# A hybrid decoder layer on one core: modulation loads issued by GpSimd's queue, later table clearing on VectorE

## The chip, the cores and the metric

The kernel runs on one core of a Trainium2 chip. The metric is device time in microseconds, the median of several runs; lower is better. The engines of the core are TensorE (PE in the profile, its weight loads PEld), VectorE (DVE), ScalarE (ACT), GpSimd (POOL) and SyncE (SP), whose instructions here are only the issues of transfers. Each engine works through its own instructions in order and waits at one until what it needs is there.

## What is computed

One layer of a decoder trunk in float32 for 256 tokens of width 2048. A conditioning vector `c` gives six modulation vectors, three for each of the two sub-layers; everything else depends on them sooner or later.

```
mod = silu(c) @ w_ada + b_ada                  # 2048 x 12288 weights, 100 MB
sh1, sc1, g1, sh2, sc2, g2 = split(mod, 6)
h = rms_norm(x, norm1_g) * (1 + sc1) + sh1
q, k, v, u = split(h @ w_in)                   # attention heads and state-space channels
attn = dilated_attention(rms_norm(q), rms_norm(k), v)
y = gelu(s5_mixer(u, ...)); ssm = y * sigmoid(y @ w_glu + b_glu)
x = x + g1 * (concat(rms_norm(attn), rms_norm(ssm)) @ w_out)
h2 = rms_norm(x, norm2_g) * (1 + sc2) + sh2
x = x + g2 * (square(relu(h2 @ w_ff1)) @ w_ff2)
```

## The kernel before, in words

**Weights.** A weight tile of 128 x 2 x 512 float32 (0.5 MB) is loaded into a slot of the tag `raw`, of which there are five (`RAW`, `raw` at L176 to L179). `load_w` and, from `w_out` on, `load_p` split it into a rounded high part `wh` on ScalarE (L161) and the remainder `wl` on VectorE (L136), each with three buffers; the matmuls (L193 to L195, L860 to L872) use both. A `raw` slot is free again when VectorE has written `wl`.

**Modulation.** The 12288 columns of `w_ada` are 24 blocks of 512, each of four pieces of 1 MB (`ada_pieces`, L246). For eight of the blocks (`PE_BLOCKS`) TensorE multiplies the pieces by the padded vector `cpad` (L254). For the others VectorE multiplies a piece by the broadcast vector `cbc` in place and sums it up (L158). `ada_raw` (L232) fetches a piece. The first eight pieces go into eight halves and wholes of tiles that are not in use yet (`first`: Q, K, U, V, TO, CA; L236). Later pieces go into the tag whose turn it is in `ring["tags"]`, a list that changes from stage to stage (`RINGS`): either a large tile that is free in that stage, as one load of 1 MB (L242), or `T0` or `raw`, as two loads of half a piece each (L244 and L178). In the second case modulation and weights share the five `raw` slots.

**The order.** `pump` (L285) advances the modulation by pieces, and `pump_at(i)` calls it between pieces of the main work at a rate from the list `PUMPS`; where a value of `mod` is needed, `pump(99, until=...)` brings it up to there. The main work is, in order: the norm of x, `make_h` and the input projection in parts (`w_in_block`, `w_in_pair`), the tables of the state space between them (`b_step`, `ca_step`, `wb_block`, `toep_half`), the scan (`state_in`, `scan`), attention and `w_glu`, `w_out`, and from about 525 us the feed-forward part (`ff1_half`, `ff1`, `ff2`). The program is written in this order; a planner then lays out each engine's own sequence from it, with its own idea of how long everything takes and of when a buffer is free, and adds the waits. All transfers are issued by the sync queue.

**Clearing.** Some tables hold zeros between written parts. GpSimd clears PD, WB0 and WB1 at the very start (L481), three parts of `toep` in the tile TO once the modulation pieces in it are used (L601), `wpad` in PD later (L492) and one column of the scan's state H in XT (L544). ScalarE then copies parts into them (`pad_write`, `toep_half`). Beyond these and four constants GpSimd has no instructions.

The functions that the change touches, with the line numbers of the profile:

Of the kernel before, what the change touches and what calls it, by code (L numbers as in the profile page):

```python
# [25 lines left out]
NB = 512  # L26
# [14 lines left out]
SUB = [0, 2, 1, 3]  # L41
# [75 lines left out]
class _K:  # L117
# [5 lines left out]
    def t(self, tag, shape, dt=F32, bufs=1):  # L123
        self.n += 1
        return self.sb.tile(list(shape), dt, name=f"{tag}_{self.n}", tag=tag, bufs=bufs)
# [5 lines left out]
    def tr(self):  # L131
        self.n += 1
        return self.ps.tile([P, NB], F32, name=f"tr_{self.n}", tag="tr", bufs=4)
# [26 lines left out]
    def copy(self, out, a, scale=1.0):  # L160
        self.last_act = self.nc.scalar.activation(out, a, AF.Copy, scale=scale).ins  # L161
# [11 lines left out]
        self.copy(hi, v)  # L173
        return self.sub(lo, v, hi.bitcast(F32))

    def raw(self, src, tag="raw"):  # L176
        raw = self.t(tag, [P, 2, NB], bufs=RAW if tag == "raw" else 1)
        self.nc.sync.dma_start(raw, src)  # L178
        return raw  # L179

    def load_w(self, src):
        parts = []
        for j in range(2):
            raw = self.raw(src[:, 2 * j : 2 * j + 2])
            hi = self.t("wh", [P, 2, NB], F32R, bufs=3)
            lo = self.t("wl", [P, 2, NB], F32R, bufs=3)
            self.split(hi, lo, raw)
            parts.append((hi, lo))
        return lambda kk: (parts[kk // 2][0][:, kk % 2, :], parts[kk // 2][1][:, kk % 2, :])
# [8 lines left out]
def _body(nc, tc, I, out, sb, ps):  # L198
    k = _K(nc, tc, I, out, (sb, ps))
# [32 lines left out]
    def ada_raw(src):  # L232
        if ring["first"] < 8:
            raw = first[ring["first"]]
            ring["first"] += 1
            nc.sync.dma_start(raw, src.rearrange("p (a n) -> p a n", a=4))  # L236
            return [raw]
        ring["i"] += 1
        tag = ring["tags"][ring["i"] % len(ring["tags"])]
        if tag not in ("raw", "T0"):  # L240
            raw = t(tag, [P, 4, NB])
            nc.sync.dma_start(raw, src.rearrange("p (a n) -> p a n", a=4))  # L242
            return [raw]
        return [k.raw(src[:, 2 * NB * i : 2 * NB * i + 2 * NB].rearrange("p (a n) -> p a n", a=2), tag) for i in range(2)]  # L244

    def ada_pieces(b):  # L246
        c4 = slice(4 * b, 4 * b + 4)
        if b in PE_BLOCKS:
            acc = tr()
            for g in range(4):  # L250
                q = 0
                for raw in ada_raw(I["w_ada"][b, g]):
                    for i in range(raw.shape[1]):
                        k.last_ada = mm(  # L254
                            acc[32 * q : 32 * q + 32, :], cpad[:, 4 * g + q, :], raw[:, i, :],
                            start=g == 0, stop=g == 3,
                        ).ins
                        q += 1
                if g < 3:
                    yield  # L260
# [6 lines left out]
        else:  # L267
            part = t("adap", [P, 2, 4], bufs=2)
            for j in range(4):
                o = 0  # L270
                for i, raw in enumerate(ada_raw(I["w_ada"][b, j])):
                    n = raw.shape[1] * NB
                    rf = raw.rearrange("p a n -> p (a n)")
                    stt(rf, rf, 1.0, cbc[:, o : o + n], ALU.mult, ALU.mult, accum=part[:, i, j : j + 1])
                    o += n
                if i:
                    add(part[:, 0, j : j + 1], part[:, 0, j : j + 1], part[:, 1, j : j + 1])
                if j < 3:
                    yield
# [94 lines left out]
    s5 = {}  # L374
# [97 lines left out]
    def pad_write(dst, src):  # L472
        for gp in range(2):
            pr = slice(64 * gp, 64 * gp + 64)
            copy(dst(gp)[pr], src[pr])
# [13 lines left out]
    def wb_block(i):  # L489
        if i == 0:  # L490
            s5["wpad"] = t("PD", [P, 8, 2, 4, 2, 16])
            nc.gpsimd.memset(s5["wpad"], 0.0)  # L492
        wpad, w, rr = s5["wpad"], i // 2, slice(8 * (i % 2), 8 * (i % 2) + 8)
        for b in range(4):
            pad_write(lambda gp: wpad[:, :, :, b, gp, :], by_r(bpow[w][:, 3 - SUB[b], :, rr]))
        wb.append(t(f"WB{i}", [P, 8, 2, P]))
        for r in range(0, 8, 2):
            pt = tr()
            for e in range(4):
                src = wpad[:, r + e // 2, e % 2].rearrange("p s g j -> p (s g j)")  # L500
                nc.tensor.transpose(pt[:, P * e : P * e + P], src, ident)
            copy(wb[i][:, r : r + 2].rearrange("p r i n -> p (r i n)"), pt)
# [38 lines left out]

    def state_in():
        H = t("XT", [P, 2, 32, 64])
        nc.gpsimd.memset(H[:, :, :, 0:1].rearrange("p i r c -> p i (r c)"), 0.0)  # L544
        for r2 in range(0, 32, 4):
            pt = tr()
            pv = pt.rearrange("p (r i c) -> p r i c", r=4, i=2)
            for r in range(r2, r2 + 4):
                for ri in range(2):
                    mm(pv[:, r - r2, ri], wb[r // 8][:, r % 8, ri], u2[:, :, r, :], start=True, stop=True)  # L550
            copy(H[:, :, r2 : r2 + 4, 1:64].rearrange("p i r c -> p r i c"), pv[:, :, :, 0:63])
        return H
# [45 lines left out]
    toep = t("TO", [P, 32, 2, 4, 16])  # L598
    for b in range(1, 4):
        tz = toep[32 * b : 32 * b + 32].rearrange("p r g s j -> p (r g) (s j)")  # L600
        nc.gpsimd.memset(tz[:, :, 0 : 16 * SUB[b]], 0.0)  # L601
    ca = t("CA", [P, 32, 2, 4, 16])
    with tc.issue_after(h_end):
        for w in range(2):
# [27 lines left out]
    for w in range(2):  # L632
        run(w_in_block(2 + w, [0, 1]), 2)
        with tc.issue_after(h_end):
            for d in range(1, 4):
                b_step(d, w, cw[:, 0], cw[:, 1])
        wb_block(2 * w)
        wb_block(2 * w + 1)
# [15 lines left out]
    for ch in range(2):  # L654
        nc.vector.transpose(u2[:, ch].rearrange("p r c -> p (r c)"), accs["u"][:, ch])
    H = state_in()
    scan()
    for n in (4, 5, 2, 3):
# [140 lines left out]
    for n in range(2):  # L799
        pz = [p[:, 0:SEQ] for p in (k.acc(), k.acc(), k.acc(), k.acc())]  # L800
        for kg in range(2):
            w = k.load_w(I["w_glu"][kg, n])
            pump_at(10)
            for kk in range(4):
                c = 4 * kg + kk
# [208 lines left out]
def _build(arrays):  # L1014
    nc = bacc.Bacc("TRN2", target_bir_lowering=False, num_devices=1)
    I = {
        n: nc.dram_tensor(n, a.shape, mybir.dt.from_np(a.dtype), kind="ExternalInput").ap() for n, a in arrays.items()
    }
    out = nc.dram_tensor("out_0_dram", (16, P, SEQ), F32, kind="ExternalOutput").ap()
    with tile.TileContext(nc, schedule_with_timeline_sim=True) as tc:  # L1020
        with tc.tile_pool(name="sb", bufs=1) as sb, tc.tile_pool(name="ps", bufs=1, space=PSUM) as ps:
            _body(nc, tc, I, out, sb, ps)
    return nc
# [9 lines left out]
```

## Time and profile before

| | |
|---|---|
| median of 3 runs | 1296.64 us (1294.19 to 1296.89) |
| the profiled execution | 1291.11 us, span 1289.3 us |
| TensorE busy | 1193.7 us, 93% |
| VectorE busy | 910.5 us, 71% |
| ScalarE busy | 579.0 us, 45% |
| GpSimd busy | 13.0 us, 1%, 12 instructions |
| bytes moved | 299.64 MB, mean 232 GB/s |
| mean granted clock of TensorE | 0.948 |

The rows come from one profiled execution, all times in microseconds from its start. A group of instructions is named by line, engine, operation and by `out<-in`, the tiles that it writes and reads. "idle before" is the time that the engine stood still in front of an instruction, with the one that ended it. In the chain of waits each step is followed back from the last instruction to what released it; "issue" there is time for which the profile shows no wait. A share of the chain tells where the end of the program was decided, a share of busy time only how much an engine did. Issues of transfers are short; the time to landing, from issue to the last byte, is given beside them.

### The profile page before, as it was taken

To read this page: it belongs to the slowest core of one execution; us is meant where nothing else is said; L and a number is where in the kernel's file an instruction comes from. 1 tells how busy PE (TensorE), PEld (TensorE's weight loads), DVE (VectorE), ACT (ScalarE), POOL (GpSimd) and SP (SyncE) were. 2 spreads that over 40 slices of the span, in tenths; PEclk is the share of its full clock that TensorE was granted. 3 is DMA by queue.
4 is the path that set the end of the run, shared out by engine and by line. 5 is a ranking of instruction groups with operands and counts; after the bars stand their busy time and mean duration, and the time that the engine had idled before them with its cause. 6 is when DMAs were issued, how large, how long until landed. Compare 5 with 4: busy or idle time off the path is not lost.

```text
span 1289.3 us, 18892 instructions
## 1 busy us (share of the span) xinstructions
PE 1193.7 (93%) x7330; PEld 1012.5 (79%) x7330; DVE 910.5 (71%) x1499; ACT 579.0 (45%) x792; POOL 13.0 (1%) x12
## 2 busy tenths in 40 slices
PE   4688899998998799789989999999999999999998
PEld 1456677863777699789978888888888888888887
DVE  5977697899534985668799655975576666667564
ACT  3588644332145544334354444453344443344432
POOL 1100000000000000000000000000000000000000
PEclk9798999997679899989999999999999999999999
DMA  9785898779155665658997666766677666767663
GB/s 371 286 317 186 280 333 287 274 267 385 36 179 180 239 193 175 210 182 297 327 326 252 203 191 216 262 212 182 195 236 240 225 187 190 219 222 227 202 212 95
DMA packets 77705, 299.64 MB, mean 232 GB/s; under 512 B 8624, under 2 KB 10928, under 8 KB 71856
## 3 DMA queue, kind: packets, MB, share of 16 engines
q1 hardware_dynamic: 77616, 298.45, 69.1%
q8 instruction: 57, 0.93, 0.3%
q14 instruction: 32, 0.26, 0.0%
HBM read 296.31 MB, written 2.10 MB: 231 GB/s over the span
## 4 chain that ended last, share of the span: by engine, by line
PE 60%; DMA 15%; DVE 15%; ACT 5%; issue 4%; SPq 0%; ACTq 0%; DVEq 0%
PE acc L860 31%; PE acc L862 15%; DMA raw<-w_ada 10%; DVE wl L136 4%; DVE raw L158 3%; DVE T L136 2%; PE acc L872 2%; PE acc L870 2%; PE acc L869 2%; PE acc L701 1%; DMA raw<-w_ff 1%; ACT wh L161 1%; PE acc L697 1%; DVE XT L136 1%; ACT TO L161 1%
## 5 line engine op out<-in xcount | busy, mean ns | idle before, releaser
L161 ACT ACTIVATE wh<-raw 128x1024 fp32r<-128x1024 f32 x360 | 381.3, 1060 | 502.1 <-PE acc L860 290.8
L136 DVE TENSOR_TENSOR wl<-raw,wh 128x1024 fp32r<-128x1024 f32 x360 | 439.7, 1223 | 219.0 <-ACT wh L161 217.2
L158 DVE SCALAR_TENSOR_TENSOR raw<-raw,cbc 128x1024 f32<-128x1024 f32 x98 | 119.6, 1225 | 49.3 <-DMA raw<-w_ada 49.0
L860 PE MATMUL acc<-CA,wh 128*128 128x512 f32 x512 | 139.7, 398 | 6.4 <-DVE rows L136 3.4
L860 PEld LDWEIGHTS acc<-CA,wh 128*128 128x128 f32 x512 | 88.4, 190 | 19.2 <-ACT wh L161 4.5
L862 PEld LDWEIGHTS acc<-CA,wl 128*128 128x128 f32 x512 | 76.7, 189 | 10.7
L862 PE MATMUL acc<-CA,wl 128*128 128x256 f32 x512 | 78.2, 278 | 0.0
L860 PE MATMUL acc<-WB,wh 128*128 128x512 f32 x256 | 70.2, 396 | 0.0
L860 PE MATMUL acc<-TO,wh 128*128 128x512 f32 x256 | 70.0, 394 | 0.0
L193 PE MATMUL acc<-wh,HA 128*128 128x512 f32 x128 | 49.8, 417 | 13.2 <-ACT HA L161 9.2
L194 PE MATMUL acc<-wl,HB 128*128 128x512 f32 x128 | 52.6, 411 | 7.1 <-DVE wl L136 7.0
L194 PE MATMUL acc<-wl,HA 128*128 128x512 f32 x128 | 53.2, 416 | 0.9 <-DVE wl L136 0.9
L195 PE MATMUL acc<-wh,HB 128*128 128x512 f32 x128 | 50.6, 400 | 0.0
L195 PE MATMUL acc<-wh,HA 128*128 128x512 f32 x128 | 50.5, 406 | 0.0
L193 PE MATMUL acc<-wh,HB 128*128 128x512 f32 x128 | 47.5, 403 | 1.7 <-ACT wh L161 1.7
L860 PEld LDWEIGHTS acc<-WB,wh 128*128 128x128 f32 x256 | 43.5, 188 | 5.6
L860 PEld LDWEIGHTS acc<-TO,wh 128*128 128x128 f32 x256 | 43.4, 188 | 5.5
L862 PEld LDWEIGHTS acc<-WB,wl 128*128 128x128 f32 x256 | 39.1, 188 | 5.9
L862 PEld LDWEIGHTS acc<-TO,wl 128*128 128x128 f32 x256 | 38.9, 188 | 5.8
L193 PEld LDWEIGHTS acc<-wh,HA 128*128 128x128 f32 x128 | 25.1, 198 | 22.4 <-ACT HA L161 9.3
L862 PE MATMUL acc<-WB,wl 128*128 128x256 f32 x256 | 40.8, 281 | 0.0
L862 PE MATMUL acc<-TO,wl 128*128 128x256 f32 x256 | 39.8, 277 | 0.0
(322 smaller groups left out, 2352.0 us busy)
## 6 DMA issues: line engine op xcount, KB each, us to landing
raw<-w_ff SPq DMA_DIRECT2D x256, 512.0 KB, 4.3
raw<-w_ada SPq DMA_DIRECT2D x98, 512.0 KB, 5.2
raw<-w_in SPq DMA_DIRECT2D x64, 512.0 KB, 6.0
raw<-w_out SPq DMA_DIRECT2D x32, 512.0 KB, 3.8
HA<-w_ada SPq DMA_DIRECT2D x11, 1024.0 KB, 7.3
PD<-w_ada SPq DMA_DIRECT2D x9, 1024.0 KB, 4.9
Q<-w_ada SPq DMA_DIRECT2D x5, 1024.0 KB, 10.3
K<-w_ada SPq DMA_DIRECT2D x5, 1024.0 KB, 8.7
```

Source lines behind the costliest of these rows:

```text
L136: return (eng or self.nc.vector).tensor_tensor(out, a, b, op=op)
L158: self.nc.vector.scalar_tensor_tensor(out, a, s, b, op0=op0, op1=op1, accum_out=accum)
L161: self.last_act = self.nc.scalar.activation(out, a, AF.Copy, scale=scale).ins
L193: mm(ps, xh, wh, start=start, stop=False)
L194: mm(ps, xh, wl, start=False, stop=False)
L195: mm(ps, xl, wh, start=False, stop=stop)
L697: mm(pv[:, r - r8], toep[:, r].rearrange("p g s j -> p (g s j)"), u2[:, :, r, :], start=True, stop=False)
L860: mm(pp[e], hi[:, e, kk], xs[kk].rearrange("p s n -> p (s n)"), start=first and kk == 0, stop=False)
L862: mm(pp[e][:, 0:SEQ], lo[:, e, kk], xs[kk][:, 0], start=False, stop=last and kk == 3)
L869: mm(o, hi[:, e, kk], xs[kk][:, 0], start=first and e + kk == 0, stop=False)
L870: mm(o, hi[:, e, kk], xs[kk][:, 1], start=False, stop=False)
L872: mm(o, lo[:, e, kk], xs[kk][:, 0], start=False, stop=last and e + kk == 4)
```

## The change

Three places in `ada_raw` and its helper `raw` issue the loads of `w_ada` on GpSimd's queue in place of the sync queue. All other transfers (x, the weights, constants, the result) stay on the sync queue. Three clearings, of `wpad`, of the column of H and of the parts of `toep`, go from GpSimd to VectorE; the clearing of PD, WB0 and WB1 at the start stays on GpSimd. Sizes, buffers, rings and rates stay as they were.

```diff
--- before.py
+++ after.py
@@ -173,9 +173,9 @@
         self.copy(hi, v)
         return self.sub(lo, v, hi.bitcast(F32))
 
-    def raw(self, src, tag="raw"):
+    def raw(self, src, tag="raw", eng=None):
         raw = self.t(tag, [P, 2, NB], bufs=RAW if tag == "raw" else 1)
-        self.nc.sync.dma_start(raw, src)
+        (eng or self.nc.sync).dma_start(raw, src)
         return raw
 
     def load_w(self, src):
@@ -233,15 +233,15 @@
         if ring["first"] < 8:
             raw = first[ring["first"]]
             ring["first"] += 1
-            nc.sync.dma_start(raw, src.rearrange("p (a n) -> p a n", a=4))
+            nc.gpsimd.dma_start(raw, src.rearrange("p (a n) -> p a n", a=4))
             return [raw]
         ring["i"] += 1
         tag = ring["tags"][ring["i"] % len(ring["tags"])]
         if tag not in ("raw", "T0"):
             raw = t(tag, [P, 4, NB])
-            nc.sync.dma_start(raw, src.rearrange("p (a n) -> p a n", a=4))
+            nc.gpsimd.dma_start(raw, src.rearrange("p (a n) -> p a n", a=4))
             return [raw]
-        return [k.raw(src[:, 2 * NB * i : 2 * NB * i + 2 * NB].rearrange("p (a n) -> p a n", a=2), tag) for i in range(2)]
+        return [k.raw(src[:, 2 * NB * i : 2 * NB * i + 2 * NB].rearrange("p (a n) -> p a n", a=2), tag, nc.gpsimd) for i in range(2)]
 
     def ada_pieces(b):
         c4 = slice(4 * b, 4 * b + 4)
@@ -489,7 +489,7 @@
     def wb_block(i):
         if i == 0:
             s5["wpad"] = t("PD", [P, 8, 2, 4, 2, 16])
-            nc.gpsimd.memset(s5["wpad"], 0.0)
+            nc.vector.memset(s5["wpad"], 0.0)
         wpad, w, rr = s5["wpad"], i // 2, slice(8 * (i % 2), 8 * (i % 2) + 8)
         for b in range(4):
             pad_write(lambda gp: wpad[:, :, :, b, gp, :], by_r(bpow[w][:, 3 - SUB[b], :, rr]))
@@ -541,7 +541,7 @@
 
     def state_in():
         H = t("XT", [P, 2, 32, 64])
-        nc.gpsimd.memset(H[:, :, :, 0:1].rearrange("p i r c -> p i (r c)"), 0.0)
+        nc.vector.memset(H[:, :, :, 0:1].rearrange("p i r c -> p i (r c)"), 0.0)
         for r2 in range(0, 32, 4):
             pt = tr()
             pv = pt.rearrange("p (r i c) -> p r i c", r=4, i=2)
@@ -598,7 +598,7 @@
     toep = t("TO", [P, 32, 2, 4, 16])
     for b in range(1, 4):
         tz = toep[32 * b : 32 * b + 32].rearrange("p r g s j -> p (r g) (s j)")
-        nc.gpsimd.memset(tz[:, :, 0 : 16 * SUB[b]], 0.0)
+        nc.vector.memset(tz[:, :, 0 : 16 * SUB[b]], 0.0)
     ca = t("CA", [P, 32, 2, 4, 16])
     with tc.issue_after(h_end):
         for w in range(2):
```

## Rows read from the trace of the kernel before

**Rows 1.** The page's first line

```profile
span 1289.3 us, 18892 instructions
```

**Rows 2.** Chain of waits over the whole span, shares by line

```profile
by line: PE acc L860 30.5%; PE acc L862 15.0%; DMA raw<-w_ada 9.6%; issue 4.4%; DVE wl L136 4.1%; DVE raw L158 2.7%; DVE T L136 2.1%; PE acc L872 1.8%; PE acc L870 1.8%; PE acc L869 1.8%; PE acc L701 1.4%; DMA raw<-w_ff 1.4%; ACT wh L161 1.
```

**Rows 3.** Stages: us; busy of PE, PEld, DVE, ACT, POOL; PEclk; DMA share; GB/s

```profile
0.00:50.00 50.00, 23.38 (x123) 9.30 (x124) 33.63 (x151) 17.48 (x36) 10.95 (x10) 0.89 0.96 381
125.00:300.00 175.00, 165.30 (x777) 129.54 (x776) 149.01 (x213) 82.08 (x115) 0.22 (x1) 0.98 0.82 288
525.00:700.00 175.00, 152.65 (x1124) 144.37 (x1124) 140.43 (x241) 73.32 (x92) 0.00 (x0) 0.94 0.80 272
700.00:1289.00 589.00, 584.37 (x3357) 509.57 (x3356) 387.22 (x521) 250.33 (x282) 0.00 (x0) 1.00 0.66 207
```

**Rows 4.** Chain of waits by line, in 125 to 300 and 525 to 700 us

```profile
by line: DMA raw<-w_ada 32.9%; issue 14.3%; DVE wl L136 12.6%; DVE raw L158 8.7%; DVE T L136 6.7%; DMA raw<-w_in 6.7%; DMA raw<-w_glu 5.7%; DVE XT L136 2.6%; DVE PD L158 2.2%; DVE WB L158 1.3%; ACT wh L161 1.2%; DVE T L158 1.2%; DVE PD L655
...
by line: DMA raw<-w_ada 32.8%; PE acc L860 11.7%; DMA raw<-w_ff 10.4%; DVE raw L158 10.2%; DVE wl L136 9.0%; issue 7.0%; PE acc L862 4.8%; ACT wh L161 3.1%; PE tr L869 2.2%; PE tr L870 2.0%; DVE rows L156 1.5%; PE tr L872 0.8%; DVE XT L156 
```

**Rows 5.** Chain of waits, 584 to 591 us: start, length, what

```profile
584.34 1.24 DVE raw L158 x2
...
585.60 5.39 DMA raw<-w_ada
```

**Rows 6.** Timeline of the sync queue: start, us, issue

```profile
584.45 1.48 SPq L178 DMA_DIRECT2D raw<-w_ada  x2
586.73 1.53 SPq L178 DMA_DIRECT2D raw<-w_ff  x2
```

**Rows 7.** The sync queue's waits, 565 to 655 us: total, times, longest

```profile
SPq L178 <- DVE wl L136: 24.4, 20, 2.3
SPq L178 <- DVE raw L158: 21.3, 21, 2.3
```

**Rows 8.** DMA issues of the page (median to landing), and issues of L178

```profile
raw<-w_ada SPq DMA_DIRECT2D x98, 512.0 KB, 5.2
...
L178 SPq DMA_DIRECT2D raw<-w_ada x98: 327/328/507, 62.7 to 1159.4; - x98
```

**Rows 9.** Timeline, clearing on POOL and DVE: start, us, idle before it

```profile
33.81 5.53 POOL L601 MEMSET TO<- 32x2048 f32 x3 [27.79 <-PE tr L254]
88.96 1.81 POOL L492 MEMSET PD<- 128x2048 f32 x1 [49.62 <-PE tr L526]
...
0.94 0.48 DVE L221 MEMSET cpad<- 128x512 f32 x1
```

**Rows 10.** Timeline of the sync queue near 410 us

```profile
410.42 0.33 SPq L178 DMA_DIRECT2D raw<-w_out  x1
410.84 11.71 SPq L242 DMA_DIRECT2D PD<-w_ada  x2
```

**Rows 11.** Timeline of VectorE and ScalarE, 68 to 78 us

```profile
68.68 1.29 DVE L136 TENSOR_TENSOR CA<-V 128x512 f32<-128x512 f32 x2
...
77.27 0.69 DVE L136 TENSOR_TENSOR cbc<-cbc,rows 128x512 f32<-128x512 f32 x1 [5.62 <-ACT rows L615]
...
70.30 3.39 ACT L161 ACTIVATE WB<-CA 64x768 f32<-64x768 f32 x4
```

**Rows 12.** Timeline of POOL and DVE, first 37 us

```profile
2.47 3.55 POOL L481 MEMSET WB<- 128x2048 f32 x2
...
3.02 3.03 DVE L152 TENSOR_SCALAR HA<-small 128x32 f32<-128x32 f32 x1 [1.42 <-DMA small<-small]
...
9.70 0.18 DVE L150 TENSOR_SCALAR HA<-HA 128x32 f32<-128x32 f32 x1
...
36.14 1.22 DVE L136 TENSOR_TENSOR wl<-raw,wh 128x1024 fp32r<-128x1024 f32 x1
```

**Rows 13.** Who waited for whom, 565 to 655 us: total, times, longest

```profile
ACT wh L161 <- DMA raw<-w_ff: 29.1, 15, 5.1
DVE raw L158 <- DMA raw<-w_ada: 11.7, 11, 3.0
```

## The prediction

> **What bounds the kernel now.** I read the page first, then the same execution by stages, then the chain of waits inside the two stages that looked loose, then the sync queue's own timeline there. The span is 1289.3 us [rows 1]. Along the chain that ended last, matmuls hold most of it, but one kind of transfer stands out: `raw<-w_ada`, the modulation loads into the five-slot ring, at 9.6% [rows 2]. The stage table says where [rows 3]. After 700 us TensorE is busy 584.37 of 589 us at a granted clock of 1.00, the 2.4 GHz level; no queue can gain there. In 125 to 300 and 525 to 700 it is busy 165.30 and 152.65 of 175 us, while the DMA engines are at 0.82 and 0.80: neither is full. In both stages a third of the chain is the same load, 32.9% and 32.8% [rows 4]. Those are the stages that this change can move, and the first 125 us, where tables are cleared.
>
> What the loose stages wait for is a ring. Modulation pieces and weights share the five `raw` slots. At 584.34 VectorE multiplies a landed piece, which frees its slot; the next load starts at 585.60 and takes 5.39 us; then again [rows 5]. The sync queue issues two modulation halves, then two weights, and the two issues of a pair, 1.48 us for both, start 1.15 us apart, which is the length of a VectorE instruction of the ring [rows 6]. The table of its waits over 565 to 655 says the same: 24.4 us for VectorE to finish a weight's low half, 21.3 us for it to finish a modulation piece [rows 7]. So the queue waits for slots to come free, in the order in which VectorE frees them. It is seldom one kind of load that holds up the other.
>
> **The change part by part, against the profiled execution.** It took 1291.11 us for a span of 1289.3; the median of the three runs is 1296.64, 5.5 us above it, and I add the sum to the median.
>
> *Modulation loads go through GpSimd.* All loads of `w_ada` move, 98 of them half pieces into the ring, with a median of 5.2 us from issue to landing; on the sync queue one issue takes 0.328 us [rows 8]. Removed from the sync queue is that issue time; it is off the chain, since the queue is waiting when it isn't issuing. Added is GpSimd's own issue, which no row shows. On the chain 9.6% of 1289.3 us is 124 us, by 5.2 us some 24 loads in a row whose length counts. Lower bound of the extra latency per load: minus 0.33 us, if GpSimd's issue were free, or minus 8 us in all. Upper bound: 1.81 us, the longest full-width GpSimd instruction [rows 9], or plus 43 us. I take 0.7 us, twice the sync queue's issue: addresses of 128 rows are far fewer words than the 2048 per partition which that clearing writes, so the price is nearer the small end. That is 17 us. Half of it I count as lost, because a load that starts later also finds less traffic in front of it (DMA share 0.8, not 1): **plus 8 us**.
>
> The Trainium skill, "DMA: Bandwidth & Descriptors", section Specifications, gives about 1 us to the first byte for a load issued by GpSimd and 0.6 us for one by the sync queue; no run here shows it yet. As an estimate from that page 24 loads would cost 10 us, and the half of them 5 us instead of my 8.
>
> *Weights alone on the sync queue.* A weight no longer stands behind a modulation load that waits, nor the other way round. In the ring this gives nothing, as read above. Among the large tiles it gives a little: at 410.42 a weight was issued that had waited, and a modulation load behind it went only 0.42 us later [rows 10]. I take minus 1 us for such places; bounds 0 and the 30 us that the second rival prices.
>
> *The start.* The DMA engines are at 0.96 and 381 GB/s in the first 50 us [rows 3]. Now modulation stands ahead of the weights in one queue; afterwards they share the engines. Five ring slots of 0.52 MB fetched meanwhile are 2.6 MB, 7 us at that rate, as the worst delay of the first eight modulation loads; against it, these no longer stand behind the 2.1 MB of `XT` (5.5 us). I take 0, with minus 5 and plus 7 as ends.
>
> *Clearing on VectorE.* Three instructions of L601 clear 64 x (16 + 32 + 48) = 6144 elements per partition; GpSimd took 5.53 us, and 1.81 us for the 2048 of L492. VectorE cleared 512 in 0.48 us [rows 9], so by that rate 5.8 and 1.9 us, and next to nothing for the 64 elements of L544. They come off GpSimd, where nothing waited for them, and join an engine which is in use. L601 needs `TO` free, which was at 33.8 us; behind it on VectorE stand the recurrence tables, the last of which (`CA`) started at 68.68 and took 1.29, and ScalarE's 3.39 us of padding read it from 70.30 on [rows 11]. So most of 5.8 us shows in ScalarE's long row of copies that follows. If they are put later, VectorE's pause of 5.62 us before 77.27 [rows 11] covers them. I take plus 4 us, bounds 0 and 7.7. L492 falls into that row of copies, which is ScalarE's, so I cost it at nothing; if VectorE is late there, its 1.9 us counts.
>
> Also, this kernel's order on every engine is laid out by a planner, which lays it out anew. I cannot see that, and put it into the width: a few us either way.
>
> Sum: 8 - 1 + 0 + 4 = plus 11 us; span about 1300, and 1296.64 + 11 = **1307.6 us**.
>
> **Rivals.** *GpSimd is locked out by VectorE.* In the first microseconds two clearings on GpSimd, 3.55 us together, ran beside a VectorE scalar operation of 128x32, which took 3.03 us where its kind takes 0.18; while L601 was cleared, a two-input subtraction took its ordinary 1.22 us [rows 12]. So the two engines do block one another, by kind of operation. If GpSimd's issues in turn waited for the VectorE instruction in progress, 24 loads would each lose up to another 1.22 us, 29 us: 1296.64 + 11 + 29 = 1337; half of it gives 1322. Against it, the ring's VectorE work is of the two-input kind that went undisturbed. Chance 0.12. The Trainium skill, "SBUF — State Buffer", section SBUF: two separate sides, states this as a rule against loads from GpSimd: while VectorE runs in a two-port mode, GpSimd can't write its descriptors and the transfer waits. The trace agrees that the port is shared (3.03 against 0.18 us), and shows it in the other direction only.
>
> *Weights run ahead: faster.* ScalarE waits 29.1 us for `raw<-w_ff` in 565 to 655 against VectorE's 11.7 us for modulation [rows 13], and of the chain in the two stages weight loads hold 6.7% and 10.4% of 175 us, 30 us [rows 4]. Had these waits come from the queue's order, separate queues would give a part back; a third is 10 us: 1296.64 - 10 = 1286.6. It decides from the point at which a weight's slot is free before the modulation loads ahead of it have been issued. Against it stand the spacing of the issues and what the queue waits for [rows 6, 7]. For it, a new order may also bring pieces forward. Chance 0.28.
>
> *Nothing shows.* The longer latency disappears in the ring's slack and the clearing in VectorE's pause: 1296.6. Against it, the loop has no slack to see [rows 5]. Chance 0.12.
>
> That the loads don't move can be left out: all three issuing lines for `w_ada` are changed, and GpSimd holds too few other instructions to be short of time.
>
> **How the numbers follow.** A measurement of this kernel can tell about 0.2%, 2.6 us, from no change. My forecast has 0.48 (its own range 1300 to 1318), the lock-out 0.12, both slower: 0.60. Nothing shows: 0.12. Weights ahead: 0.28. The range goes from 1284, which takes in most of the faster case, to 1328, where the issue price nears 1.8 us; a tenth is left out at each end.
>
> **What would show it.** Right: `raw<-w_ada` issued by GpSimd with a median to landing nearer 6 than 5.2 us; the sync queue's waits in 565 to 655 still for VectorE; TensorE busy less than 165 and 153 us per 175; three clearings of about 5.8 us on VectorE before 70 us and ScalarE's padding of `CA` later than 70.30. The last 589 us unchanged. Wrong: landings as short as before, or weights that land before ScalarE asks for them in these stages; or, for the lock-out, GpSimd's issues that end only when a VectorE instruction does.

## The result and the profile after

The changed kernel takes **1328.15 us** (median of four runs, 1323.48 to 1332.84) against 1295.41 for the kernel before (1293.43 to 1296.89, four runs): ratio 1.0254, 95% interval 1.0207 to 1.0301. It is slower by 33 us; forecast were 11, to 1307.6, and the range ended at 1328, a little below the result. The profiled execution of after took 1332.84 us, among the longer of its runs, and that of before 1291.11, so the two traces differ by 41.8 us of span; some 9 us of that are this pair's own.

The runs of the kernel before fall into two groups, 16 of 84 at 1278.6 to 1285.4 us with a mean granted clock of 0.961 to 0.968 and the others at 1289.8 to 1301.4 us with 0.943 to 0.956, so a difference of 10 us can be this and not an edit, and edits are read here by stretches of the traces, with medians as the total.

The page and the stages, of the kernel after; columns as in [rows 1, 3, 8]:

```profile
span 1331.1 us, 19023 instructions
...
raw<-w_ada POOLq DMA_DIRECT2D x98, 512.0 KB, 5.3
```

```profile
0.00:50.00 50.00, 17.10 (x66) 3.90 (x66) 23.41 (x119) 12.51 (x25) 10.79 (x17) 0.90 0.96 382
125.00:300.00 175.00, 161.67 (x765) 131.78 (x765) 140.84 (x207) 87.12 (x130) 19.02 (x36) 0.96 0.77 264
525.00:700.00 175.00, 147.46 (x1174) 143.23 (x1173) 116.40 (x190) 68.67 (x87) 19.00 (x36) 0.92 0.72 237
700.00:1331.00 631.00, 622.92 (x3563) 542.14 (x3562) 425.51 (x589) 266.69 (x300) 14.79 (x28) 1.00 0.68 211
```

```profile
L178 POOL DMA_DIRECT2D raw<-w_ada x98: 527/527/537, 84.0 to 1201.6; - x98
```

Three readings. A modulation load into the ring now costs GpSimd 0.527 us to issue, never more than 0.537, where the sync queue took 0.328 [rows 8]; from the start of the issue to landing it takes 5.3 us, before 5.2. The last stage is TensorE's as before. And the first 50 us, for which I had entered 0, hold 17.10 us of matmul where there were 23.38 [rows 3], at the same DMA share and rate.

There the trace shows what stands in the way. ScalarE, the kernel after (start, us, instruction, idle time before it and what ended that):

```profile
22.95 1.06 ACT L161 ACTIVATE wh<-raw 128x1024 fp32r<-128x1024 f32 x1 [15.44 <-DMA raw<-w_in]
26.74 1.06 ACT L161 ACTIVATE wh<-raw 128x1024 fp32r<-128x1024 f32 x1 [2.73 <-DMA raw<-w_in]
27.70 0.71 ACT L302 ACTIVATE rows<-XT 128x256 f32<-128x256 f32 x2
...
40.62 1.06 ACT L161 ACTIVATE wh<-raw 128x1024 fp32r<-128x1024 f32 x1 [9.08 <-DMA raw<-w_in]
41.58 0.71 ACT L302 ACTIVATE rows<-XT 128x256 f32<-128x256 f32 x2
...
49.30 0.42 ACT L165 ACTIVATE HB<-HB 128x256 f32<-128x256 f32 x1
```

The splits of the first weights (L161) stand among the squares of the norm (L302) and wait for their loads. The norm's square root (L165) comes at 49.30. In the kernel before it came at 31.59, behind squares that ran in one row from 21.18, and the first split followed it:

```profile
21.18 0.72 ACT L302 ACTIVATE rows<-XT 128x256 f32<-128x256 f32 x2 [15.01 <-PE tr L305]
...
31.59 0.42 ACT L165 ACTIVATE HB<-HB 128x256 f32<-128x256 f32 x1
32.09 1.06 ACT L161 ACTIVATE wh<-raw 128x1024 fp32r<-128x1024 f32 x1
```

VectorE, the kernel after, and ScalarE's wait behind it:

```profile
53.25 5.45 DVE L136 TENSOR_TENSOR XT<-XT,rbc 128x256 f32<-128x256 f32 x16
58.62 0.15 DVE L136 TENSOR_TENSOR mod<-tr,small 128x4 f32<-128x4 f32 x1
59.25 1.76 DVE L601 MEMSET TO<- 32x2048 f32 x1 [0.48 <-PE tr L254]
61.27 0.91 DVE L601 MEMSET TO<- 32x1024 f32 x1 [0.25 <-issue]
62.86 2.62 DVE L601 MEMSET TO<- 32x3072 f32 x1 [0.68 <-issue]
65.51 0.16 DVE L156 SCALAR_TENSOR_TENSOR g1c<-mod,small 128x4 f32<-128x4 f32 x1
65.59 0.15 DVE L136 TENSOR_TENSOR mod<-tr,small 128x4 f32<-128x4 f32 x1
```

```profile
65.77 2.07 ACT L324 ACTIVATE XT<-XT,mod,g1c 128x256 f32<-128x256 f32 x4 [10.03 <-DVE mod L136]
```

The clearing, 5.29 us where 5.8 was costed from [rows 9], stands between the norm and the scale `g1c`. Behind it comes the last sum for `mod`, and ScalarE waits 10.03 us until that is done before it makes the input of the first projection. So the first matmul of that projection starts at 68.21 instead of 46.40.

The whole difference by stretches, from the starts of the same instructions in each trace (us). "Scan" runs from VectorE's transposes of `u` (L655) to the first GLU matmul (L809), less the state product inside it (L701), which has its own column; "ff" from the first matmul of the attention output (L869 on `CA`) to the first of L860 on `WB`.

```
                                first   to L655  scan   L701   GLU   ff     to the
                                matmul                                      last L860
before                          46.4    181.2    110.4  34.5   54.9  294.0  563.2
after                           68.2    178.8    120.9  36.4   57.2  301.7  563.3
first 8 back on sync            56.0    174.1    119.8  36.4   58.5  301.4  562.9
clearing back on GpSimd         63.8    175.2    118.1  36.4   58.3  300.4  563.3
both back                       48.5    178.5    119.9  36.3   56.4  300.3  563.8
before, clearing on VectorE     52.6    181.4    110.0  34.6   53.0  297.1  563.8
before, first 8 on GpSimd       58.5    182.2    109.0  34.8   58.3  294.5  563.5
before, large tiles on GpSimd   48.2    178.7    118.9  36.3   56.9  289.5  566.4
before, ring on GpSimd          45.5    186.2    112.2  27.9   56.2  302.8  564.1
all loads on GpSimd             45.3    180.2    112.4  28.0   56.4  298.1  563.5
all, clearing on VectorE        52.4    180.9    113.4  36.4   54.0  297.0  563.8
ring wholly on GpSimd           50.5    180.2    112.5  29.1   57.7  298.4  565.2
first 8 on ScalarE's queue      45.6    184.3    108.8  21.8   55.9  293.5  564.0
first 8 on GpSimd, order held   50.1    181.7    110.1  36.2   58.7  291.2  562.4
after, splits alone held        66.1    180.7    125.6  36.4   55.8  300.4  563.9
after, again                    69.0    178.0    120.2  36.4   56.0  303.0  564.2
after, order held               59.0    182.9    117.5  36.4   57.0  301.7  563.5
after, order held, again        59.7    183.1    117.3  36.4   57.4  303.8  563.9
the same, clearing on GpSimd    54.2    180.1    119.1  36.4   58.5  298.0  564.1
```

After against before: start +21.8, scan +10.5, ff +7.7, the rest +1.9; together 41.9, the difference of the traces.

### The profile page after: what moved, and what is told of

Read it like the earlier page. It is cut to its first block, busy times and chain, and to the rows that moved or that the text cites. A ratio compares the mean times of both kernels' runs of the same rounds, so it can differ in the third digit from the quotient of the medians.

```text
span 1331.1 us, 19023 instructions
## 1 busy us (share of the span) xinstructions
PE 1199.6 (90%) x7330; PEld 1017.1 (76%) x7330; DVE 920.8 (69%) x1504; ACT 581.0 (44%) x794; POOL 83.7 (6%) x155
## 4 chain that ended last, share of the span: by engine, by line
PE 56%; DMA 12%; issue 8%; DVE 7%; ACT 1%; POOL 0%; POOLq 0%; DVEq 0%; ACTq 0%
PE acc L860 28%; PE acc L862 14%; DMA raw<-w_ada 7%; DVE wl L136 2%; PE acc L869 2%; PE acc L870 2%; PE acc L872 2%; PE acc L701 1%; DVE T L136 1%; DMA raw<-w_ff 1%; PE acc L697 1%; DMA HB<-consts 1%; DVE raw L158 1%; DMA PD<-w_ada 1%; PE tr L254 1%
## 5 line engine op out<-in xcount | busy, mean ns | idle before, releaser
L161 ACT ACTIVATE wh<-raw 128x1024 fp32r<-128x1024 f32 x360 | 380.7, 1060 | 538.4 <-PE acc L860 273.2
L860 PE MATMUL acc<-CA,wh 128*128 128x512 f32 x512 | 141.5, 402 | 9.0 <-ACT wh L161 5.0
L860 PEld LDWEIGHTS acc<-CA,wh 128*128 128x128 f32 x512 | 89.3, 192 | 22.5 <-ACT wh L161 5.2
L178 POOL DMA_DIRECT2D raw<-w_ada x98 | 51.7, 528 | 787.7 <-DVE wl L136 366.1
L860 PE MATMUL acc<-TO,wh 128*128 128x512 f32 x256 | 69.9, 395 | 0.4 <-DVE rows L136 0.4
L860 PE MATMUL acc<-WB,wh 128*128 128x512 f32 x256 | 70.0, 396 | 0.0
L860 PEld LDWEIGHTS acc<-TO,wh 128*128 128x128 f32 x256 | 43.4, 188 | 6.1 <-issue 0.6
L860 PEld LDWEIGHTS acc<-WB,wh 128*128 128x128 f32 x256 | 43.6, 188 | 5.7
L862 PE MATMUL acc<-WB,wl 128*128 128x256 f32 x256 | 40.6, 281 | 0.0
```

The lines of the kernel that those rows point to most:

```text
L178: (eng or self.nc.sync).dma_start(raw, src)
L860: mm(pp[e], hi[:, e, kk], xs[kk].rearrange("p s n -> p (s n)"), start=first and kk == 0, stop=False)
L862: mm(pp[e][:, 0:SEQ], lo[:, e, kk], xs[kk][:, 0], start=False, stop=last and kk == 3)
```

## The experiments

**Which edit costs what.** First the changed kernel with one edit undone, and the kernel before with one made.

```diff
 # e1_first_sync, in the changed kernel
-            nc.gpsimd.dma_start(raw, src.rearrange("p (a n) -> p a n", a=4))   (L236)
+            nc.sync.dma_start(raw, src.rearrange("p (a n) -> p a n", a=4))
 # e2_clear_gpsimd in the changed kernel: its three later nc.vector.memset back to nc.gpsimd.memset
 # e3_clear_only in the kernel before: those three to nc.vector.memset
```

> The changed kernel with only its first eight modulation loads (the 8 MB of the start) back on the sync queue. Theory S (the loss is made at the start: modulation and the first weights share the DMA engines, the weights land later than the planner laid out, and ScalarE, in order, waits for them in front of the norm's squares): the squares run in one row again, the first input-projection matmul comes at about 51 us in place of 68.21, and the time falls by about 17 us, from 1328 to about 1311. Theory R (the loss is in the ring of five slots, spread over all loads, as I had forecast): the start moves little or its gain is not kept, 1323 or more.

Measured: 1313.39 us (1.0151, 1.0116 to 1.0187), 15 below the changed kernel; first matmul at 56.0. The start is nearly half of the loss.

> The changed kernel with the three clearings back on GpSimd. Theory C (VectorE's clearing of three parts of TO stands in front of the last modulation add, for 6 us): the first input-projection matmul comes at about 62 us in place of 68.21 and the time falls by about 6 us, to 1322. Rival: on GpSimd the clearings stand behind two modulation loads that wait for their tiles, so the tables that need them are late by as much, and the time stays at 1328 within 3 us.

Measured: 1322.36 (1.0222, 1.0191 to 1.0252), 6 below; first matmul 63.8.

> The kernel before with only the three clearings moved to VectorE, all loads on the sync queue. Theory C: the clearings stand in front of the last modulation add, the first input-projection matmul comes 3 to 6 us after 46.4 us and the time rises by as much, from 1295.4 to 1298 to 1302. Rival (VectorE has time to spare there, the add was late anyway): within 2 us of 1295.4.

Measured: 1290.29 (0.9984, 0.9942 to 1.0026). By the median the clearing is free; the trace doesn't bear that out, for the first matmul is 6.2 us late and the rest of the trace is 1.8 us longer, not shorter. Three of the four runs lay at a granted clock of 0.964 to 0.965 and took 1287.9 to 1291.3, where the kernel before took at most 1285.4 at 0.961 to 0.968; the fourth took 1299.08 at 0.951. So the clearing did cost, some 6 us by the trace, and a higher clock hid it in the median.

Then the three sets of loads, each alone: L236 (first eight), L242 (large tiles), L178/L244 (ring halves), and the last two together.

```diff
 # e5_later_gpsimd: the changed kernel, with e1's and e2's edits
 # e6_first_gpsimd: the kernel before, with L236 alone on nc.gpsimd
 # e7_big_gpsimd: the kernel before, with L242 alone on nc.gpsimd
 # e8_ring_gpsimd: the kernel before, with k.raw(..., tag, nc.gpsimd) in L244 alone
```

> The changed kernel with its first eight modulation loads back on the sync queue and its three clearings back on GpSimd, so that only the later modulation loads are on GpSimd's queue. Theory S (most of the loss is the first 50 us, where the modulation tiles take bandwidth from the tables and the first weights): the first matmul of the input projection starts at 48 to 51 us (46.4 before, 56.0 with the clearings on VectorE), and the time is 1304 to 1310, 10 to 15 us above the kernel before, since what is lost behind 300 us stays. Theory R (the later loads cost nothing; what is left of the loss in the earlier run with the first eight on the sync queue was the clearings): 1291 to 1297.

> The kernel before with only its first eight modulation loads on GpSimd's queue. Theory S: the tables land at 25 to 31 us after their issue as in the changed kernel, the first matmul of the input projection starts at 60 to 64 us, and most of that stays to the end: 1305 to 1313. Rival (the late start is absorbed by the waits behind it, as the 6 us of the clearings were when they alone were moved): first matmul as late, but 1293 to 1299.

> The kernel before with only the loads of the large modulation tiles (HA, U, WB, PD and the like) on GpSimd's queue; the first eight and the small-tile loads stay on the sync queue, the clearings on GpSimd. Theory L (what is lost behind 300 us is the large tiles' doing: they share the DMA engines with the pattern load of HB in front of the scan): HB's load takes 14 to 15 us to landing in place of 7.8, the first step of the scan product comes 4 to 8 us later against the state projection than before, and the time is 1299 to 1306. Theory Q (the small-tile loads do it, behind in-order waits on GpSimd): 1290 to 1297.

> The kernel before with only the small-tile modulation loads (the ring of raw tiles) on GpSimd's queue, the large ones and the first eight on the sync queue. Theory L: GpSimd's issue of 0.53 us shows nowhere, landing stays at 5.2 to 5.4 us, the stretch from 125 to 300 us is as long as before within 2 us, and the time is 1291 to 1297. Theory Q (in-order waits on GpSimd and the longer issue cost what my prediction's ring term said, or what is lost behind 300 us): 1299 to 1306.

Measured: e5 1313.38 (1.0145, 1.0082 to 1.0207); e6 1308.93 (1.0113, 1.0052 to 1.0173); e7 1298.38 (1.0049, 1.0011 to 1.0087); e8 1301.84 (1.0078, 1.0037 to 1.0119). Against 1293.99 the three sets alone cost 14.9, 4.4 and 7.8 us, 27 in sum; with 6 for the clearing, that is the changed kernel's 33. That the sum fits is luck: the large tiles and the ring together (e5) cost 19, not 12. In e8's trace the state product took 27.9 us instead of 34.5, by the clock (last section); without that column its trace is 17 us longer than that of the kernel before. Each set shows chiefly in its own stretch: the first eight in the start (58.5), the large tiles in the scan (118.9 against 110.4), the ring in ff (302.8 against 294.0) and, alone, ahead of L655 too (186.2 against 181.2). The first theory missed in e5: the start was whole again (48.5), yet 1313, since the later loads cost what I had given the start. One part of the scan's loss has a row of its own: the load of the pattern in `HB`, which VectorE needs in the midst of the scan. In the kernel before and in the changed one (KB, median us to landing):

```profile
HB<-consts SPq DMA_DIRECT2D x1, 384.0 KB, 7.8
```

```profile
HB<-consts SPq DMA_DIRECT2D x1, 384.0 KB, 15.2
```

In the chain after, this load alone is 15.23 us from 323.92. VectorE stands still for it for 3.0 us there; in the kernel before it had landed 3 us ahead of its use. In e7 it takes 12.6, and VectorE waits 0.18 us for it, though the scan is 8.5 us longer. So this load explains a part in the changed kernel and next to nothing in e7; the rest isn't explained here.

```profile
339.17 1.03 DVE L156 SCALAR_TENSOR_TENSOR HB<-HB 128x384 f32<-128x384 f32 x2 [3.00 <-DMA HB<-consts]
```

**Is it GpSimd's queue?** All loads there, and all of the ring there.

```diff
 # e9_all_gpsimd: the kernel before, every nc.sync.dma_start of an input to nc.gpsimd.dma_start
 # e10_ring_all_gpsimd: the kernel before, one line (L178)
-        self.nc.sync.dma_start(raw, src)
+        self.nc.gpsimd.dma_start(raw, src)
```

> The kernel before with every load (small tables, x, modulation, weights) on GpSimd's queue and none on the sync queue, so that there is one queue in one order again, but it is GpSimd's. Theory O (two queues lose the order of one: each load shares the DMA engines, and the ring of five tiles, with loads that were behind it): the first matmul of the input projection starts at 46 to 50 us, the pattern load of HB lands in 7 to 10 us, the stretch from the first transpose of the feed-forward weights to the second block's first product (169 us before, 179 in the changed kernel) is 167 to 172, and the time is 1292 to 1301. Theory G (it is GpSimd's queue itself: 0.53 us an issue against 0.33, and whatever else it adds to each load): the start is 10 us or more late, that stretch is 179 or longer, 1308 to 1330.

> The kernel before with all loads of the ring of raw tiles, of weights and of modulation, on GpSimd's queue; the tables, x and the large modulation tiles stay on the sync queue. With only the modulation's ring loads there the time was 1301.8, 7.8 above the kernel before. Theory O (the ring's loss is that its five tiles are refilled by two queues, each waiting in its own order): one queue for the ring gives it back, the stretch from the first transpose of the feed-forward weights to the second block's first product is 167 to 172 us (180.5 with the modulation's loads alone), 1292 to 1299, unless the first weights, now on another queue than the tables, make the start late, which the first matmul of the input projection shows (46.4 before). Theory G (GpSimd's issue in each refill of the ring): with all the refills there the loss doubles, 1305 to 1320.

Measured: e9 **1288.47** (0.9972, 0.9939 to 1.0005), e10 1302.21 (1.0106, 1.0042 to 1.0171). With one queue again the start is that of before (45.3) and the scan nearly (112.4), though every load, weights included, is issued by GpSimd at 0.53 us: GpSimd's queue is not what costs there. Nor is its lower median a gain: in its trace the state product took 28.0 us where the kernel before took 34.5, by the clock. In the ring GpSimd's queue may cost a part: ff is 298.1 and 298.4 in these two (297.0 in e11 below), 294.0 before, 302.8 in e8. That would be 4 us for the longer issue and 4 for the two queues; but the kernels whose ring is on the sync queue spread from 289.5 to 297.1, and those with two queues from 298.0 to 303.8, so the split is indicated, not shown. I had expected ff to fall back wholly, which it did not. e10's time stands between the two theories; its tables and x are again on another queue than the first weights, and its start is 4 us late.

How the two queues meet in the ring can be read from the waits of 550 to 730 us, in the kernel before and in e8 (us in total, times, longest):

```profile
DVE raw L158 <- DMA raw<-w_ada: 12.7, 13, 3.0
...
SPq L178 <- DMA raw<-w_ada: 10.1, 9, 2.6
```

```profile
DVE raw L158 <- DMA raw<-w_ada: 24.6, 19, 4.1
...
SPq L178 <- DMA raw<-w_ada: 29.5, 10, 8.2
```

The five slots are still one ring. With two queues the sync queue's weights wait for slots that modulation loads of the other queue still fill, and VectorE waits twice as long for modulation.

**Two more, both missed.**

```diff
 # e11_all_clear: e9, with the three later clearings on nc.vector
 # e12_first_scalar: the kernel before, with L236 alone on nc.scalar.dma_start
```

> The kernel with every load on GpSimd's queue (1288.5 in its own runs, ratio 0.9972), and the three later clearings on VectorE as in the change. GpSimd's clearing of TO stands there at 35.48 us, 5.47 us long, between two weight loads. If a clearing on the queue's own engine holds loads that the path waits for, taking it off gives 2 to 6 us: 1283 to 1287, ratio under 0.996, and this would be the version that beats both kernels. If the clearing costs VectorE what it gives GpSimd: 1287 to 1292, ratio 0.996 to 1.000.

> The kernel before with its first eight modulation loads issued by ScalarE's queue, and all else on the sync queue: two queues at the start as in the run with these eight on GpSimd's (first matmul of the input projection at 58.5 us, 1308.9), but GpSimd has no part in it. Theory O (two queues, whichever they are): first matmul at 55 to 62 us, the first weights' splits again ahead of the squares on ScalarE, 1302 to 1312. Theory G (GpSimd's queue has a part in the late start): first matmul at 46 to 50, 1291 to 1298.

Measured: e11 1305.2 (1.0125, 1.0071 to 1.018), 17 above e9; e12 1292.2 (0.9991, 0.9945 to 1.0036). In e11 the clearing stands on VectorE from 39.74 to 45.96, between the pieces of the norm's product on `XT`; the first matmul is 7.1 us later than in e9. Another 8.4 lie in the state product, 36.4 us against 28.0, and that is TensorE's clock (last section). e12 overthrew my theory that any second queue costs at the start: two queues share the engines there, and the first matmul comes at 45.6. The sync queue's waits over the first 40 us, e12 and then the changed kernel:

```profile
SPq L209 <- DMA Q<-w_ada: 3.7, 1, 3.7
```

```profile
SPq L609 <- DMA XT<-xT: 4.4, 1, 4.4
```

The sync queue's issues wait there for the landing of a load that ScalarE issued, and the first weights leave at 10.12 us; in e6 and after they wait for the sync queue's own loads only and leave at 3.2. The planner's order on ScalarE then is nearly the old one: the squares come first but for one split at 27.07, whose load had landed at 25.5.

**Bandwidth or order?** Held back in e4: the splits. In e13: the splits and the product of `dskip` with the identity table. In e15 the clearing is on GpSimd as well.

```diff
 # e4_norm_first, in the changed kernel: load_w's split behind the last square root on ScalarE
+            with self.tc.issue_after(self.last_sqrt):
-            self.split(hi, lo, raw)
+                self.split(hi, lo, raw)
 # e13_first_gpsimd_order: e6 with that hold (on the first square root), and on VectorE
+    with tc.issue_after(rbc_end):
-    mul(dskip, ident4...
+        mul(dskip, ident4...
 # e14_after_order, e17_after_order_again: the changed kernel with both; e16_after_again: the changed kernel
 # e15_after_order_clear: e14, with the three later clearings on nc.gpsimd
```

> The changed kernel with one ordering edge: ScalarE's splits of weights come behind the square root of the first norm, as they stood before the change; queues and loads as in the change. Theory S, by order: ScalarE no longer waits for weights in front of the squares, the square root comes at about 32 us in place of 49.30, the first input-projection matmul at about 53 us, the time falls to about 1313. Theory S, by bandwidth alone (the modulation pieces themselves land too late because the engines are shared): the first matmul stays at 62 us or later and the time at 1322 or more.

Measured: 1322.22 (1.0241, 1.0189 to 1.0293); the square root at 44.23, the first matmul at 66.1, only 2 us earlier. By the expectation this spoke for bandwidth, but VectorE shows another reason (e4):

```profile
43.43 0.42 DVE L136 TENSOR_TENSOR dskip<-ident,small 128x256 f32<-128x256 f32 x1 [22.05 <-DMA ident<-consts]
43.78 0.41 DVE L150 TENSOR_SCALAR HB<-tr 128x256 f32<-128x256 f32 x1
```

The next waiting instruction in the queue ahead of the norm took the first one's place.

> The kernel before with its first eight modulation loads on GpSimd's queue, as in the run that took 1308.9 (first matmul of the input projection at 58.5 us), and with the first weights' splits on ScalarE and the dskip product on VectorE held behind the norm's square root and reciprocal. Theory P (the planner's order on ScalarE and VectorE, waits for loads ahead of the norm): the square root comes at 30 to 34 us (46.2 in that run, 31.6 before), the first matmul at 46 to 49, and the time is 1290 to 1298. Theory S (the loads land late, since two queues share the DMA engines): square root may come early, but the first matmul stays at 54 us or later, 1302 to 1310.

> The changed kernel with the same two holds (splits and dskip behind the norm), all else as changed. Theory P: the first matmul of the input projection comes at 50 to 55 us (68.2 in the changed kernel; the clearing on VectorE, 4 to 7 us, stays), and the time is 1309 to 1317, the start's share of the loss. Theory S: first matmul at 62 us or later, 1320 to 1330.

Measured: e13 **1297.21** (1.0026, 0.9976 to 1.0076), 12 below e6; square root at 29.9, first matmul at 50.1. ScalarE in e13:

```profile
29.91 0.42 ACT L165 ACTIVATE HB<-HB 128x256 f32<-128x256 f32 x1
...
36.47 1.06 ACT L161 ACTIVATE wh<-raw 128x1024 fp32r<-128x1024 f32 x1 [4.26 <-DMA raw<-w_in]
```

The loads' queues are those of e6. So at e6's start the loss is chiefly the order on ScalarE and VectorE, not bandwidth: 8.4 of 12.1 us come back. The 3.7 us that stay go with a third split, which still waits 4.26 us for its load ahead of the norm's next step on VectorE. In the changed kernel something is added: the third of the first weights and the identity table land at 40.6 and 43.1, 4 to 5 us later than in e6, while two large modulation tiles that GpSimd issued at 11.7 and 15.4 are in flight beside them. That e15's first matmul (54.2) is 4 us behind e13's fits this; no run tests it alone. e14: 1326.61 (1.0271, 1.0192 to 1.035), with the first matmul at 59.0 and the trace 8.5 us shorter than after, but the median, of another set of runs, only 1.5.

> The changed kernel once more, beside the next two on one chip: 1323 to 1333, as in its own runs.

> The changed kernel with the first weights' splits and the dskip product held behind the norm, beside the changed kernel itself. Theory P (what the order costs at the start stays to the end): 6 to 10 us below the changed kernel's median on this chip, as the profiled executions showed (8.5). Rival (a later wait takes it back): within 3 us of it.

> The same holds, and the three clearings back on GpSimd: of the change only the queue of the modulation loads is left, with the start mended. Theory P: first matmul of the input projection at 49 to 53 us, and 1308 to 1317, as with only the later loads on GpSimd (1313.4): what is left, 13 to 20 us above the kernel before, is the later loads'. Rival (a later wait takes it back): 1318 or more.

Measured on one chip: e16 1330.25 (1.0302, 1.0239 to 1.0364), e17 1328.01 (1.0301, 1.0235 to 1.0366), e15 1314.36 (1.019, 1.0129 to 1.025). In the whole change the rival holds for the order alone: of 9.3 us won at the first matmul, 5.1 are lost again by L655 (183.1 against 178.0), and the medians differ by 2. With the clearing off VectorE too, 16 us come back, about as in e1 and e5. What takes the 5 us back I haven't settled. Nor are the parts independent in that kernel: e1 alone gave 15 us, e2 alone 6, both together (e5) 15.

None of these kernels beats the kernel before beyond its interval; the nearest is e9.

## Why the prediction was right and wrong

- **The sign was right; that the ring's term fits is luck.** I entered plus 8 us from a guessed extra latency of 0.7 us for each of 24 loads. Alone the ring costs 7.8 (e8, with the clock's help), 7.7 in ff after. But from issue to landing, the longer issue included, a load takes 5.3 us where it took 5.2; by my own working that would be 2.4 us at most, and landings as short as before were my sign of being wrong. In its place e8 shows two queues that refill one ring: the sync queue's issues wait 29.5 us for modulation loads instead of 10.1. How much of the loss is this and how much the longer issue, the runs leave open (e9 and e10 point to half and half). "Weights alone", minus 1, was of the wrong sign: I read [rows 7] as a queue that seldom makes one kind wait for the other, and didn't ask who would wait once each kind had its own order.
- **The clearing**, plus 4 of 0 to 7.7: 6 us (e2; 6.2 and 7.1 at the first matmul in e3 and e11), though with the first eight back on the sync queue it shows in no median (e1 and e5). The durations were right; the place was wrong. It did not fall beside the tables of [rows 11] but ahead of `g1c`, on the path of the first matmul. I took the place where `TO` comes free in the old order as its place in the new one.
- **The start is the step that failed**: I entered 0, with minus 5 and plus 7 as ends, from bytes and rate alone. It is 15 us (e1, e6). The rate was in fact the same, 382 against 381 GB/s. In e6 the identity table landed about as early (38.1 us, before 39.0); x landed later (19.6 against 10.8), but it did so in e13 as well (19.0), where most of the start was won back. What changed is the order that the planner lays out. In e6 and after, the first weights leave at 3.2 us instead of 13.4, and their splits, and `dskip`, are placed ahead of the norm, where the splits wait for landings while squares that need only x stand behind them. Shown by e13 for e6; in the changed kernel holding the order won 9.3 us at the first matmul and 2 in the time. I had named the planner and given it "a few us".
- **A term was missing**: the large tiles. I priced [rows 10] as a gain of 1; they cost about 8 us in the scan (117.3 to 120.9, and 125.6 in e4, in the table's kernels that have them on another queue than the load of `HB`; 108.8 to 113.4 in the others), 4.4 in e7's median. All later loads together, for which I had entered 7, cost 19 (e5).
- **Weights run ahead** (0.28): at the start they did, and that made it slower. In the feed-forward part they did not: over 597 to 687, about the same work as in [rows 13], ScalarE waited 40.3 us for weights where it had waited 29.1, and VectorE 21.0 for modulation where it had waited 11.7.

```profile
ACT wh L161 <- DMA raw<-w_ff: 40.3, 15, 5.1
...
DVE raw L158 <- DMA raw<-w_ada: 21.0, 15, 3.1
```

- **Lock-out** (0.12): not borne out. No issue of 98 lasted over 0.537 us, and landing took 5.3 us against 5.2; that the measured time lies between its 1322 and 1337 is chance. The rule of the Trainium skill, "SBUF — State Buffer", section SBUF: two separate sides, that a load from GpSimd must wait while VectorE runs in a two-port mode, shows in no row of the ring; whether VectorE runs in such a mode there no run tells.
- **Nothing shows** (0.12): refuted by the result.
- A measurement of this kernel does not tell 2.6 us from no change, as I had it: its runs lie between 1278.6 and 1301.4.
- Loads that change queues meet others. The identity table, 80 KB, took 8.2 us to land before and 23.9 after; issued 11.6 us earlier, it landed 4 us later. The Trainium skill, "DMA: Bandwidth & Descriptors", section Queues, rings and completion order, says that each DMA engine takes turns between the queues that have work; this agrees with it. The Trainium skill, "DMA: Bandwidth & Descriptors", section Issuing engines are not separate DMA queues, has it that several issuing engines only save issue time. Here they saved none that shows in a time, and changed who waits for whom: 33 us with the clearing.

## What to carry to other kernels

A single queue is also a schedule: it holds back what is needed later. Before moving part of its loads to a second queue, list for each engine which instructions will stand ahead of the critical ones and what they wait for, and, where a planner writes that order, compare the orders before pricing the bytes. Moving a part of the loads of a shared ring cost 9 us of ff here, moving all of them 4: rather all, or none, as far as these runs indicate it. And where the granted clock differs from run to run, compare stretch by stretch.

## What the runs showed of the hardware

**TensorE's clock decides 13 us of the state product.** The kernel before and e12, windows over L701's products (columns as in [rows 3]; the clock is the third number from the end):

```profile
340.00:350.00 10.00, 10.00 (x88) 8.12 (x88) 0.00 (x0) 0.60 (x1) 0.00 (x0) 0.50 0.01 2
350.00:360.00 10.00, 10.00 (x88) 8.23 (x88) 0.00 (x0) 0.60 (x1) 0.00 (x0) 0.50 0.00 0
```

```profile
330.00:340.00 10.00, 8.79 (x124) 7.01 (x121) 9.86 (x27) 2.46 (x9) 0.00 (x0) 1.00 0.18 74
340.00:350.00 10.00, 10.00 (x147) 8.31 (x146) 2.06 (x4) 1.19 (x2) 0.00 (x0) 1.00 0.01 2
```

At 0.50, the 1.2 GHz level, the product takes 34.5 us; at 1.00, 2.4 GHz, 21.8; with a rise on the way 28. TensorE was busy throughout at 0.50. In the 10 us ahead of these windows' start it had been busy 10.00 us at 0.60 in the kernel before (330 to 340) and 9.90 us at 0.60 in e12 (320 to 330). The times of one kernel differ by about as much: three of e12's runs, at a mean clock of 0.960 to 0.965, took 1278.3 to 1282.2 us, the others, at 0.947 to 0.954, 1291.3 to 1295.0. Its trace is one of the former (1280.41); that of the kernel before has 0.948 and 1291.11. That this product makes the difference fits, but no kernel was profiled at both, and what decides the level stays open.

**A load's issue can wait for another engine's load.** With the first eight on ScalarE's queue, the sync queue's loads of x waited 3.7 us for one of theirs; with these on GpSimd's queue no wait of x, the first weights or the tables names one of the eight. I had not expected the two to differ. These waits are the planner's, and the traces show their pattern: no issue of the sync queue, of 539 in the kernel before and 391 after, starts before the load that it issued eight places earlier has landed. Before, the first weight was its 14th load and left at 13.38, just when the sixth, a modulation load, had landed; after, it is the sixth and leaves at 3.15. This gives the planner weights to place ahead of the norm. It fits the 17 us between e12 and e6; that it is the reason was not tested apart from the order.
